# mLSTM state recurrence: one backward pass for both directions' state contributions, the forward state carried along in the output pass

## The chip, the core and the metric

The kernel runs on one core of a Trainium2 chip. The metric is the device time of one execution in microseconds, the median of several runs. One core has five engines with an instruction queue each: TensorE (PE: matrix products and transposes), VectorE (DVE), ScalarE (ACT), GpSimd (POOL) and SyncE (SP, which here issues most DMA transfers). They run side by side and wait for each other through semaphores. SBUF is the on-chip memory, PSUM the small memory into which PE writes and from which DVE and ACT can read.

## The reference, cut to what matters

Two layers of a hybrid block with three token mixers side by side: Fourier, bidirectional mLSTM, attention. 1024 latent and 256 context tokens, width 1024, all in float32. The change is in the mLSTM alone: 4 heads of dimension 96, run forward and backward over the tokens, context first in both. In layer 0 the context tokens' outputs are needed too, in layer 1 (the last) only the latents'.

```python
def mlstm_chunkwise(q, k, v, li, lf, state):
    def step(carry, inp):
        C, n, m = carry
        ...
        s = jnp.einsum("bhtd,bhsd->bhts", qb, kb) * w_intra
        num = jnp.einsum("bhts,bhsv->bhtv", s, vb) + w_inter[..., None] * jnp.einsum("bhtd,bhdv->bhtv", qb, C)
        den = s.sum(axis=-1) + w_inter * jnp.einsum("bhtd,bhd->bht", qb, n)
        h = num / jnp.maximum(jnp.abs(den), jnp.exp(-m_t))[..., None]
        ...
        C_new = decay[..., None, None] * C + jnp.einsum("bhs,bhsd,bhsv->bhdv", wk, kb, vb)
        n_new = decay[..., None] * n + jnp.einsum("bhs,bhsd->bhd", wk, kb)
        return (C_new, n_new, m_new), h
...
        fwd_c, bwd_c = mlstm_inputs(mqc, mkc, mvc, mgc, conv_qk[l], b_gates[l])
        fwd, bwd = mlstm_inputs(mq, mk, mv, mg, conv_qk[l], b_gates[l])
        hcf, st_f = mlstm_direction(fwd_c, zero, False)
        hcb, st_b = mlstm_direction(bwd_c, zero, True)
        hf, _ = mlstm_direction(fwd, st_f, False)
        hb, _ = mlstm_direction(bwd, st_b, True)
        y_m = mlstm_output(hf, hb, mo, g_mlstm[l])
```

## The kernel before

The kernel cuts the 1280 tokens into ten chunks of 128: 0 to 7 are latents, 8 and 9 context. `order[0]` is the forward order 8, 9, 0, ..., 7, and `order[1]` the backward order 9, 8, 7, ..., 0. The state of a head and direction is a 96x97 matrix: C, and n as its 97th column, since v has a column of ones. The stabilisers, weights (`wkT`) and decays (`decb`) of all chunks are worked out earlier, so that only sums and products of C are left here.

`mlstm()` is a Python generator with two passes.

The **state pass** (L825 to L853) takes 9 positions x 2 directions = 18 steps a layer. One step loads the keys of a chunk (`kc`, 96 x 4 x 128) and its values (`vc`), transposes the four heads' keys on PE (L834) into a PSUM tile, copies it with ACT into `tm` (L836), multiplies the values by the weights on POOL (L839, into a buffer with the tag `Mb`), and forms four products of 97 columns on PE (L842) in a second PSUM tile. DVE adds decay times previous state, head by head (L850, which reads the product from PSUM; the states use the tags `qw` forward and `Wb` backward), and the new state is written to DRAM (`dC`, L852). After each step the generator yields.

The **output pass** (from L875) takes a chunk at a time, 0 to 9 in layer 0 and 0 to 7 in layer 1. It loads keys, queries (`qc`), values and the output gate (`mo`), forms the scores of four heads (L885), and copies them (L887, `ssb`). Then, for each direction, it loads the masks `Mb` and `Wb` (L896), builds the weights with POOL (L897), ACT and DVE (L901, `tm`), scales the queries on POOL (L906, `qw`), loads the state before the chunk (`Cp`), and accumulates the outputs of weights and state in one PSUM tile (L912, L914). DVE divides them by the denominator: `dn` (L918 to L920) and `hd` (L922). The sum of both directions is normalised by `tail()` (L854 to L872) one chunk later: a POOL sum (L856), a small Newton iteration for the root on DVE (L175 to L187), the products L863 and L865 (`mo`), and three transposes on PE (L868).

None of this runs by itself. The generator is side work of the attention: the list `bg` at the start of the attention stage pulls it once between each of 23 pieces (keys, the first block's queries, its twelve score tiles L1005 with their maxima L1006, the row maximum L1012 and L1015, values). Then the loop over key tiles (L1140 scores, L1142 exponential, L1143 product with the values) calls `side_work()`, which pulls it at a rate set by a quota (`nm_`, the expected count of steps). Both use the PSUM tag `l`, of which there are two tiles. The order on each engine is decided when the program is built, by a list scheduler with priorities; the engines then run their queues in order.

Tags matter in what follows: a tile with a tag takes one of `bufs` buffers, and waits for the last use of the tile that had the buffer before. The state pass and the output pass share `kc`, `vc`, `tm`, `Mb`, `qw` and `Wb`, two buffers each.

Of the kernel before, what the change touches and what calls it, by code (L numbers as in the profile page):

```python
# [9 lines left out]
ALU = mybir.AluOpType  # L10
# [53 lines left out]
def build(tc, A, out, dbg=None):  # L64
    nc = tc.nc
# [40 lines left out]
    V, S, G, PE = nc.vector, nc.scalar, nc.gpsimd, nc.tensor  # L106
# [12 lines left out]
    ident = T(cst, [128, 128], tag="cst")  # L119
# [98 lines left out]
    dC = DT("dC", [2, 10, 96, 388])  # L218
# [206 lines left out]
    order = [[8, 9, 0, 1, 2, 3, 4, 5, 6, 7], [9, 8, 7, 6, 5, 4, 3, 2, 1, 0]]  # L425

    late, R1 = [], [None]
    for l in range(2):
# [286 lines left out]
        def tok(ci):  # L715
            return slice(ci * 128, (ci + 1) * 128)
# [96 lines left out]
        def mlstm(mlp_):  # L813
# [8 lines left out]

            dkh = dk.rearrange("(h d) t -> d h t", h=4)
            dqh = dq.rearrange("(h d) t -> d h t", h=4)
            prev = [None, None]  # L825
            for p in range(9):
                for d in range(2):
                    ci = order[d][p]
                    kc = T(mlp_, [96, 4, 128], tag="kc", bufs=2)
                    nc.sync.dma_start(kc, dkh[:, :, tok(ci)])  # L830
                    vc = load_v(ci)
                    ps = T(psL, [128, 512], tag="l")
                    for h in range(4):
                        PE.transpose(ps[:, h * 96:(h + 1) * 96], kc[:, h, :], ident[:96, :96])  # L834
                    kt = T(mlp_, [128, 512], tag="tm", bufs=2)
                    S.copy(kt[:, :384], ps[:, :384])  # L836
                    wcol = wkT[:, 64 * d + ci:64 * d + ci + 31:10]
                    wv = T(mlp_, [128, 4, 128], tag="Mb", bufs=2)
                    G.tensor_tensor(wv[:, :, :97], vc, wcol.unsqueeze(2).to_broadcast([128, 4, 97]), ALU.mult)  # L839
                    pc = T(psL, [128, 512], tag="l")  # L840
                    for h in range(4):
                        PE.matmul(pc[:96, h * 97:(h + 1) * 97], kt[:, h * 96:(h + 1) * 96], wv[:, h, :97], start=True, stop=True)  # L842
                    C = T(mlp_, [96, 4, 128], tag=("qw", "Wb")[d], bufs=2)
                    pv = pc[:96, :388].rearrange("p (h e) -> p h e", h=4)
                    if p == 0:
                        S.copy(C[:, :, :97], pv)
                    else:
                        for h in range(4):
                            dcol = 40 * d + 10 * h + ci
                            V.scalar_tensor_tensor(C[:, h, :97], prev[d][:, h, :97], decb[:, dcol:dcol + 1], pv[:, h], ALU.mult, ALU.add)  # L850
                    prev[d] = C
                    nc.sync.dma_start(dC[d, ci].rearrange("p (h e) -> p h e", h=4), C[:, :, :97])  # L852
                    yield  # L853
            def tail(ci, hs, mo):  # L854
                hsum = hs[0]
                G.tensor_tensor(hsum, hs[0], hs[1], ALU.add)  # L856
# [15 lines left out]
                nc.sync.dma_start(dy[256:640].rearrange("(i p) t -> p i t", p=128)[:, :, tok(ci)], ym)  # L872

            pend = None
            for ci in range(10 if ctx_all else 8):  # L875
                kc = T(mlp_, [96, 4, 128], tag="kc", bufs=2)
                nc.sync.dma_start(kc, dkh[:, :, tok(ci)])
                qc = T(mlp_, [96, 4, 128], tag="qc", bufs=2)
                nc.sync.dma_start(qc, dqh[:, :, tok(ci)])
                vc = load_v(ci)  # L880
                mo = T(mlp_, [128, 384], tag="mo", bufs=2)
                nc.sync.dma_start(mo, dv[tok(ci), 384:768])
                sp = T(psL, [128, 512], tag="l")
                for h in range(4):
                    PE.matmul(sp[:, h * 128:(h + 1) * 128], kc[:, h, :], qc[:, h, :], start=True, stop=True)  # L885
                ssb = T(mlp_, [128, 512], tag="ssb")
                S.copy(ssb, sp)  # L887
                yield
                hs = []
                for d in range(2):  # L890
                    Mb = T(mlp_, [128, 4, 128], tag="Mb", bufs=2)
                    Wb = T(mlp_, [96, 4, 128], tag="Wb", bufs=2)
                    for src, dst, np_ in ((dM, Mb, 128), (dW, Wb, 96)):
                        v_ = src[64 * d:64 * d + 40].rearrange("(h c) t -> h c t", h=4)[:, ci, :]
                        nc.sync.dma_start(dst, v_.unsqueeze(0).to_broadcast([np_, 4, 128]))
                    tm = T(mlp_, [128, 4, 128], tag="tm", bufs=2)  # L896
                    G.tensor_tensor(tm, msk[:, d].unsqueeze(1).to_broadcast([128, 4, 128]), Mb, ALU.subtract)  # L897
                    for h in range(4):
                        col = 64 * d + 10 * h + ci
                        S.activation(tm[:, h], tm[:, h], AF.Exp, bias=aT[:, col:col + 1])  # L900
                    V.tensor_tensor(tm.rearrange("p h t -> p (h t)"), tm.rearrange("p h t -> p (h t)"), ssb, ALU.mult)  # L901
                    first = ci == order[d][0]
                    if not first:
                        pi = order[d][order[d].index(ci) - 1]
                        qw = T(mlp_, [96, 4, 128], tag="qw", bufs=2)
                        G.tensor_tensor(qw, qc, Wb, ALU.mult)  # L906
                        Cp = T(mlp_, [96, 4, 97], tag="Cp", bufs=2)
                        nc.sync.dma_start(Cp, dC[d, pi].rearrange("p (h e) -> p h e", h=4))
                    po = T(psL, [128, 512], tag="l")
                    for h in range(4):  # L910
                        o = po[:, h * 97:(h + 1) * 97]
                        PE.matmul(o, tm[:, h], vc[:, h], start=True, stop=first)  # L912
                        if not first:
                            PE.matmul(o, qw[:, h], Cp[:, h], start=False, stop=True)  # L914
                    pv = po[:, :388].rearrange("p (h e) -> p h e", h=4)
                    dn = T(mlp_, [128, 4], tag="dn", bufs=2)
                    fl = flT[:, 64 * d + ci:64 * d + ci + 31:10]
                    V.scalar_tensor_tensor(dn, pv[:, :, 96], -1.0, fl, ALU.mult, ALU.max)  # L918
                    V.tensor_tensor(dn, pv[:, :, 96], dn, ALU.max)
                    V.reciprocal(dn, dn)  # L920
                    hd = T(mlp_, [128, 4, 96], tag=f"hd{d}", bufs=2)
                    V.tensor_tensor(hd, pv[:, :, 0:96], dn.unsqueeze(2).to_broadcast([128, 4, 96]), ALU.mult)  # L922
                    hs.append(hd)
                    yield
                    if d == 1 and pend is not None:
                        tail(*pend)
                        yield
                pend = (ci, hs, mo)
# [175 lines left out]
                        quota["g"] = None  # L1104
                        break

        nm_ = 18 + 4 * (10 if ctx_all else 8) - len(bg) + 1
        nf_ = (7 if ctx_all else 4) * 2 + 1
        quota = dict(m=0.0, f=0.0, g=None, rm=nm_ / (tot * RM[l]), rf=nf_ / (tot * RF))
        ending = None  # L1110
# [593 lines left out]
```

## Time and profile before

| | us |
|---|---|
| median of 3 runs | 3073.31 (3073.06 to 3073.51) |
| profiled execution, its own time | 3063.51 |
| its span, first to last instruction | 3061.7 |
| granted PE clock, mean | 0.960 |
| attention stage of layer 0: first state transposes (L834) | at 360.41 |
| first mask product of its output pass (L897) | at 424.88 |
| the same two in layer 1 | at 1966.31 and 2042.04 |
| last transposes of `tail()` in layer 1 (L868) | at 2171.3 |

The profile is of one execution. A row of a timeline gives start and length in us, engine, source line, operation, what it writes and reads, shape and count, and in brackets how long the engine had been idle ahead of it and what ended that. A table of windows gives, for each stretch, the busy time of every engine out of its length (with the number of instructions), the granted PE clock and the DMA share. `PE` is the product stream, `PEld` the loads of weights, which run beside it. A float32 product appears as two records on PE, so that `x8` is a group of four. Lines of the kernel before are L1 to L1703; the changed kernel has its own numbers, higher by up to 27 in this part.

### The profile page before, as it was taken

What the parts mean: (1) busy time and instruction counts of PE and PEld (TensorE: products, weight loads), DVE (VectorE), ACT (ScalarE), POOL (GpSimd) and SP (SyncE); (2) the same over time, 40 slices, a digit from 0 to 9 for tenths busy, and PEclk for the clock granted to TensorE, in tenths of its full rate; (3) what the DMA queues carried; (4) which work ended last, traced back from release to release, by engine and by line L of the source; (5) the groups of instructions that cost most, each with busy time, mean ns of one, the idle gap of its engine ahead of it and who ended that gap; (6) DMA issues with size and microseconds to landing.
All of it is one profiled execution on the core that took longest, in us unless ns stands there. A gap on an engine that the chain in (4) does not pass through costs nothing. (4 is left out here: it accounts for less than half of the span.)

```text
span 3061.7 us, 40347 instructions
## 1 busy us (share of the span) xinstructions
PE 2861.2 (93%) x14152; PEld 2306.0 (75%) x14152; DVE 1982.2 (65%) x3708; ACT 1176.6 (38%) x2283; POOL 1050.2 (34%) x935
## 2 busy tenths in 40 slices
PE   7998989989989999999999999899999899989996
PEld 7887866656768888788887787866657688868885
DVE  7769567632488767777777627448533854468887
ACT  3322244442343333333344533245333543434444
POOL 4212133111464444221225333224123675413334
PEclk7999998999989999999999999899999899999998
DMA  6514576223335444732121212455134343352321
GB/s 233 165 58 134 144 171 163 83 82 104 114 132 197 161 154 152 285 117 90 55 93 40 111 42 84 118 146 154 61 101 137 121 147 115 108 196 92 110 90 55
DMA packets 277871, 376.43 MB, mean 123 GB/s; under 512 B 63396, under 2 KB 154468, under 8 KB 276004
## 3 DMA queue, kind: packets, MB, share of 16 engines
q1 hardware_dynamic: 274788, 366.51, 38.1%
q0 software_dynamic: 576, 4.20, 0.4%
q10 hardware_dynamic: 2304, 3.15, 0.3%
q8 instruction: 112, 1.84, 0.2%
q14 instruction: 91, 0.75, 0.1%
HBM read 283.74 MB, written 90.02 MB: 122 GB/s over the span
## 5 line engine op out<-in xcount | busy, mean ns | idle before, releaser
L138 PE MATMUL mm<-A,wr 128*128 128x512 f32 (+1 forms) x840 | 316.5, 379 | 19.0 <-ACT rb L673 10.8
L135 PE MATMUL mm<-A 128*128 128x512 f32 (+1 forms) x654 | 251.0, 389 | 10.9 <-DVE A L148 8.5
L136 PE MATMUL mm<-A 128*128 128x512 f32 (+1 forms) x654 | 242.8, 387 | 0.3 <-DVE A L148 0.3
L134 PE MATMUL mm<-A 128*128 128x512 f32 (+1 forms) x654 | 237.6, 387 | 5.7 <-ACT A L147 4.5
L148 POOL TENSOR_TENSOR wr<-wf,wr 128x512 fp32r<-128x512 f32 x88 | 122.0, 1396 | 258.8 <-ACT wr L147 199.9
L143 PE MATMUL mm<-A,wr 128*128 128x512 f32 (+1 forms) x520 | 196.1, 378 | 4.6 <-POOL A L148 2.1
L138 PEld LDWEIGHTS mm<-A,wr 128*128 128x128 f32 x840 | 161.5, 193 | 51.5 <-ACT rb L673 12.5
L138 PE MATMUL mm<-A,c 128*128 128x512 f32 (+1 forms) x520 | 184.3, 356 | 15.4 <-ACT c L147 13.3
L144 PE MATMUL mm<-A,wr 128*128 128x512 f32 (+1 forms) x520 | 193.5, 373 | 0.0
L1143 PE MATMUL v<-PT,Vt 128*97 128x512 f32 (+1 forms) x336 | 176.7, 610 | 12.5 <-ACT PT L1142 12.5
L143 PE MATMUL mm<-A,c 128*128 128x512 f32 (+1 forms) x520 | 184.9, 356 | 3.1 <-DVE A L148 2.3
L144 PE MATMUL mm<-A,c 128*128 128x512 f32 (+1 forms) x520 | 183.9, 354 | 0.8 <-DVE c L148 0.8
L235 DVE SCALAR_TENSOR_TENSOR junk<-wf,t 128x512 bf16<-128x512 f32 x192 | 131.3, 684 | 74.0 <-DMA wf<-in_w_mt 70.6
L1140 PE MATMUL s<-Q,KT 97*128 97x512 f32 (+1 forms) x336 | 174.0, 606 | 0.4 <-ACT Q L1016 0.4
L147 ACT ACTIVATE A<-wr 128x512 fp32r<-128x512 f32 x188 | 114.2, 625 | 147.7 <-PE mm L135 59.2
L147 ACT ACTIVATE A<-A 128x512 fp32r<-128x512 f32 x174 | 106.9, 625 | 158.3 <-PE mm L135 85.1
L1142 ACT ACTIVATE PT<-s 128x512 f32<-128x512 f32 (+1 forms) x168 | 97.9, 584 | 153.7 <-PE s L1140 153.3
L148 DVE TENSOR_TENSOR A<-wr,A 128x512 fp32r<-128x512 f32 x146 | 128.3, 891 | 42.8 <-ACT A L147 27.7
L135 PEld LDWEIGHTS mm<-A 128*128 128x128 f32 x654 | 123.4, 189 | 39.5 <-DVE A L148 11.9
L134 PEld LDWEIGHTS mm<-A 128*128 128x128 f32 x654 | 122.7, 188 | 31.1 <-ACT A L147 7.0
L136 PEld LDWEIGHTS mm<-A 128*128 128x128 f32 x654 | 123.5, 189 | 24.8 <-DVE A L148 0.7
L138 PE MATMUL mm<-wr,A 128*128 128x256 f32 x464 | 134.0, 289 | 6.6 <-ACT rb L673 4.7
(481 smaller groups left out, 8016.8 us busy)
## 6 DMA issues: line engine op xcount, KB each, us to landing
wf<-in_w_mt SPq DMA_DIRECT2D x96, 256.0 KB
x<-in_w_up SPq DMA_DIRECT2D x40, 512.0 KB
r<-in_w_up SPq DMA_DIRECT2D x38, 512.0 KB
wr<-in_w_dn SPq DMA_DIRECT2D x36, 512.0 KB
gt<-in_w_mt SPq DMA_DIRECT2D x64, 256.0 KB
da<-wf SPq DMA_DIRECT2D x64, 256.0 KB
da<-p SPq DMA_DIRECT2D x64, 256.0 KB
wf<-in_w_in SPq DMA_DIRECT2D x56, 256.0 KB
```

The source lines that it names most:

```text
L134: PE.matmul(ps, lh, rh, start=first, stop=False, skip_group_check=True)
L135: PE.matmul(ps, lh, rl, start=False, stop=False, skip_group_check=True)
L136: PE.matmul(ps, ll, rh, start=False, stop=last, skip_group_check=True)
L138: PE.matmul(ps, lh, rh, start=first, stop=False)
L143: PE.matmul(ps, lh, rl, start=False, stop=False)
L144: PE.matmul(ps, ll, rh, start=False, stop=last)
L147: (hi or S).activation(dst[0], src, AF.Copy) if (hi is None or hi is S) else hi.tensor_copy(dst[0], src)
L148: (lo or G).tensor_tensor(dst[1], src, f32(dst[0]), ALU.subtract)
L235: V.scalar_tensor_tensor(junk, f, 1.0, cb[w], ALU.mult, ALU.mult, accum_out=(ga, modT[l])[kh][:, w, j:j + 1])
L1140: PE.matmul(ps[:, :nq], K[:, tok(kt)], Q[:, :nq], start=True, stop=True)
L1142: S.activation(PT[:, :nq], ps[:, :nq], AF.Exp, scale=scale)
L1143: PE.matmul(po[:97, :nq], Vt[kt // 2][:, kt % 2, h % 2], PT[:, :nq], start=i == 0, stop=i == len(kts) - 1)
```

## The change

The state pass now takes the ten chunks once, in backward order. For each it makes one load of keys and values, one set of transposes, two POOL products (one for each direction, side by side in a tile with its own tag, `wv`), and four PE products of 194 columns in two PSUM tiles. The forward half of each product, not yet summed, is copied by ACT (`fw`, tag `Cp`, now four buffers) and written to `dC[0, ci]`. The backward half is summed with the decayed state as before (L853, tag `Cf`) and written to `dC[1, ci]`. It yields twice a chunk.

The forward state is summed up in the output pass by `forward()`: it loads the chunk's contribution from `dC[0, ci]` and adds decay times the state so far with four DVE instructions (L869), whose tensors all lie in SBUF. It is called behind the products of direction 0. So that the state is at hand, the output pass of layer 0 now runs in the order 8, 9, 0, ..., 7; in layer 1, which has no outputs for 8 and 9, `forward()` runs for these two ahead of the loop.

Per layer there are 10 state steps in place of 18: 40 transposes in place of 72, 40 products of 194 columns in place of 72 of 97, 10 loads of kc and vc each in place of 18, 20 POOL products in place of 18, 32 DVE instructions that read PSUM in place of 64, 32 new ones that read SBUF alone, and 20 ACT copies of forward halves that are new.

```diff
-            prev = [None, None]
-            for p in range(9):
+            prev = None
+            for ci in order[1]:
+                kc = T(mlp_, [96, 4, 128], tag="kc", bufs=2)
+                nc.sync.dma_start(kc, dkh[:, :, tok(ci)])
+                vc = load_v(ci)
...
+                wv = T(mlp_, [128, 4, 2, 97], tag="wv", bufs=2)
                 for d in range(2):
...
                     wcol = wkT[:, 64 * d + ci:64 * d + ci + 31:10]
-                    wv = T(mlp_, [128, 4, 128], tag="Mb", bufs=2)
-                    G.tensor_tensor(wv[:, :, :97], vc, wcol.unsqueeze(2).to_broadcast([128, 4, 97]), ALU.mult)
+                    G.tensor_tensor(wv[:, :, d], vc, wcol.unsqueeze(2).to_broadcast([128, 4, 97]), ALU.mult)
+                yield
+                fw = T(mlp_, [96, 4, 97], tag="Cp", bufs=4)
+                C = T(mlp_, [96, 4, 97], tag="Cf", bufs=2)
+                for hp in range(2):
                     pc = T(psL, [128, 512], tag="l")
-                    for h in range(4):
-                        PE.matmul(pc[:96, h * 97:(h + 1) * 97], kt[:, h * 96:(h + 1) * 96], wv[:, h, :97], start=True, stop=True)
-                    C = T(mlp_, [96, 4, 128], tag=("qw", "Wb")[d], bufs=2)
...
+                    pv = pc[:96, :388].rearrange("p (h d e) -> p h d e", h=2, d=2)
+                    for h in range(2 * hp, 2 * hp + 2):
+                        PE.matmul(pc[:96, 194 * (h % 2):194 * (h % 2) + 194], kt[:, h * 96:(h + 1) * 96], wv[:, h].rearrange("p d e -> p (d e)"), start=True, stop=True)
+                    S.copy(fw[:, 2 * hp:2 * hp + 2], pv[:, :, 0])
+                    if prev is None:
+                        S.copy(C[:, 2 * hp:2 * hp + 2], pv[:, :, 1])
+                    elif ci:
+                        for h in range(2 * hp, 2 * hp + 2):
+                            dcol = 40 + 10 * h + ci
+                            V.scalar_tensor_tensor(C[:, h], prev[:, h], decb[:, dcol:dcol + 1], pv[:, h % 2, 1], ALU.mult, ALU.add)
+                if ci != 7:
+                    nc.sync.dma_start(dC[0, ci].rearrange("p (h e) -> p h e", h=4), fw)
+                if ci:
+                    nc.sync.dma_start(dC[1, ci].rearrange("p (h e) -> p h e", h=4), C)
+                prev = C
+                yield
+
+            def forward(ci, C):
+                lc = T(mlp_, [96, 4, 97], tag="Cp", bufs=4)
+                nc.sync.dma_start(lc, dC[0, ci].rearrange("p (h e) -> p h e", h=4))
+                if C is None:
+                    return lc
+                n_ = T(mlp_, [96, 4, 97], tag="Cf", bufs=2)
+                for h in range(4):
+                    dcol = 10 * h + ci
+                    V.scalar_tensor_tensor(n_[:, h], C[:, h], decb[:, dcol:dcol + 1], lc[:, h], ALU.mult, ALU.add)
+                return n_
...
-            for ci in range(10 if ctx_all else 8):
+            Cf = None
+            if not ctx_all:
+                for ci in order[0][:2]:
+                    Cf = forward(ci, Cf)
+            for ci in order[0] if ctx_all else order[0][2:]:
...
-                        Cp = T(mlp_, [96, 4, 97], tag="Cp", bufs=2)
-                        nc.sync.dma_start(Cp, dC[d, pi].rearrange("p (h e) -> p h e", h=4))
+                        if d:
+                            Cp = T(mlp_, [96, 4, 97], tag="Cp", bufs=4)
+                            nc.sync.dma_start(Cp, dC[d, pi].rearrange("p (h e) -> p h e", h=4))
+                        else:
+                            Cp = Cf
...
+                    if d == 0 and ci != 7:
+                        Cf = forward(ci, Cf)
...
-        nm_ = 18 + 4 * (10 if ctx_all else 8) - len(bg) + 1
+        nm_ = 20 + 4 * (10 if ctx_all else 8) - len(bg) + 1
```

Three places show how the queues move. The first is PE's queue at the start of the attention stage of layer 0: `l_...` are PSUM tiles of the mLSTM, `m_...` those of attention, and a row is an instruction, or a run of them, in the order of its queue (the score tiles L1005 are left out). Before:

```order
L834 MATMUL l_3497<-cst_60,kc_3492 128x96 x4
...
L842 MATMUL l_3506<-Mb_3504,tm_3502 96x97
L834 MATMUL l_3548<-cst_60,kc_3543 128x96 x4
L842 MATMUL l_3506<-Mb_3504,tm_3502 96x97 x3
...
L842 MATMUL l_3557<-Mb_3555,tm_3553 96x97 x4
L834 MATMUL l_3576<-cst_60,kc_3571 128x96 x4
...
L842 MATMUL l_3585<-Mb_3583,tm_3581 96x97
L834 MATMUL l_3607<-cst_60,kc_3602 128x96 x4
L842 MATMUL l_3585<-Mb_3583,tm_3581 96x97 x3
L842 MATMUL l_3616<-Mb_3614,tm_3612 96x97 x4
L834 MATMUL l_3638<-cst_60,kc_3633 128x96 x4
L1015 MATMUL m_4037<-cst_60,m_746_4035 1x128
```

After (L832 is the transpose, L846 the product, L1032 the score tile, L1042 the row maximum's transpose):

```order
L832 MATMUL l_3497<-cst_60,kc_3492 128x96 x4
L1032 MATMUL m_3645<-x_588_3481,Qr_3615 128x512
...
L1032 MATMUL m_3830<-x_588_3481,Qr_3615 128x512
L846 MATMUL l_3538<-wv_3504,tm_3502 96x194 x2
L846 MATMUL l_3543<-wv_3504,tm_3502 96x194 x2
L1032 MATMUL m_3848<-x_588_3481,Qr_3615 128x256
L832 MATMUL l_3561<-cst_60,kc_3556 128x96 x4
L1042 MATMUL m_3869<-cst_60,m_701_3867 1x128
```

Ahead of the row maximum stood four groups of products and five of transposes; now there are one chunk's products and two groups of transposes, and eleven of the twelve score tiles stand ahead of the products.

The second is SP's queue at the same place, with the loads of keys (`kc`), values (`vc`) and the output pass's masks (`Mb`, `Wb`). Before:

```order
L830 DMA kc_3492<-dk_80 96x4x128
L830 DMA kc_3543<-dk_80 96x4x128
...
L820 DMA vc_3545<-dv_81 128x4x96
L830 DMA kc_3571<-dk_80 96x4x128
L820 DMA vc_3494<-dv_81 128x4x96
```

After:

```order
L917 DMA Mb_3941<-dM_89 128x4x128
L917 DMA Mb_3973<-dM_89 128x4x128
L917 DMA Wb_3942<-dW_90 96x4x128
L828 DMA kc_3492<-dk_80 96x4x128
L828 DMA kc_3556<-dk_80 96x4x128
L901 DMA qc_3919<-dq_79 96x4x128
L917 DMA Wb_3974<-dW_90 96x4x128
L820 DMA vc_3558<-dv_81 128x4x96
L820 DMA vc_3494<-dv_81 128x4x96
```

The first masks of the output pass are now loaded ahead of the first keys.

The third is DVE's queue in one chunk of the output pass of layer 0. `dn` is the denominator and `hd` the output of one direction, `y` the Newton iterate, `mo` the product of the chunk before, and `mx` the maxima of attention. Before:

```order
L918 SCALAR_TENSOR_TENSOR dn_4697<-l_4688,flT_1253 128x4
L185 TENSOR_TENSOR rs_t_4797<-y_962_4793 128x4
L919 TENSOR_TENSOR dn_4697<-l_4688,dn_4697 128x4
L186 TENSOR_TENSOR rs_t_4797<-rs_t_4797,rs_h_4794 128x4
L920 RECIPROCAL dn_4697<-dn_4697 128x4
L187 SCALAR_TENSOR_TENSOR y_962_4793<-rs_t_4797,y_962_4793 128x4
L922 TENSOR_TENSOR hd_936_4701<-l_4688,dn_4697 128x384
```

After:

```order
L945 SCALAR_TENSOR_TENSOR dn_4604<-l_4588,flT_1253 128x4
L869 SCALAR_TENSOR_TENSOR Cf_4755<-Cf_4599,decb_1254,Cp_4753 96x97 x4
L1033 TENSOR_REDUCE mx_5048<-m_5049 128x1
L883 SCALAR_TENSOR_TENSOR mo_4367<-mo_4367,hd_862_4424 128x384
L946 TENSOR_TENSOR dn_4604<-l_4588,dn_4604 128x4
L945 SCALAR_TENSOR_TENSOR dn_4646<-l_4637,flT_1253 128x4
...
L947 RECIPROCAL dn_4604<-dn_4604 128x4
...
L949 TENSOR_TENSOR hd_912_4608<-l_4588,dn_4604 128x384
```

The four instructions of the forward state stand between the first and the second instruction of the denominator of direction 0, ahead of the product `mo` of the chunk before.

More of the change, by code (lines that the diff above doesn't have):

```diff
@@ L824, in mlstm @@
             dqh = dq.rearrange("(h d) t -> d h t", h=4)
-            prev = [None, None]
-            for p in range(9):
-                for d in range(2):
[L828 to L832, printed above, removed]
-                    for h in range(4):
-                        PE.transpose(ps[:, h * 96:(h + 1) * 96], kc[:, h, :], ident[:96, :96])
-                    kt = T(mlp_, [128, 512], tag="tm", bufs=2)
-                    S.copy(kt[:, :384], ps[:, :384])
-                    wcol = wkT[:, 64 * d + ci:64 * d + ci + 31:10]
-                    wv = T(mlp_, [128, 4, 128], tag="Mb", bufs=2)
-                    G.tensor_tensor(wv[:, :, :97], vc, wcol.unsqueeze(2).to_broadcast([128, 4, 97]), ALU.mult)
-                    pc = T(psL, [128, 512], tag="l")
-                    for h in range(4):
-                        PE.matmul(pc[:96, h * 97:(h + 1) * 97], kt[:, h * 96:(h + 1) * 96], wv[:, h, :97], start=True, stop=True)
-                    C = T(mlp_, [96, 4, 128], tag=("qw", "Wb")[d], bufs=2)
[L844 to L853, printed above, removed]
@@ new lines, in mlstm @@
+            prev = None
[3 more added lines that the diff above has]
+                vc = load_v(ci)
+                ps = T(psL, [128, 512], tag="l")
+                for h in range(4):
+                    PE.transpose(ps[:, h * 96:(h + 1) * 96], kc[:, h, :], ident[:96, :96])
+                kt = T(mlp_, [128, 512], tag="tm", bufs=2)
+                S.copy(kt[:, :384], ps[:, :384])
+                wv = T(mlp_, [128, 4, 2, 97], tag="wv", bufs=2)
+                for d in range(2):
+                    wcol = wkT[:, 64 * d + ci:64 * d + ci + 31:10]
+                    G.tensor_tensor(wv[:, :, d], vc, wcol.unsqueeze(2).to_broadcast([128, 4, 97]), ALU.mult)
[3 more added lines that the diff above has]
+                for hp in range(2):
+                    pc = T(psL, [128, 512], tag="l")
+                    pv = pc[:96, :388].rearrange("p (h d e) -> p h d e", h=2, d=2)
[14 more added lines that the diff above has]
+                yield
@@ new lines, in forward @@
+            def forward(ci, C):
[4 more added lines that the diff above has]
+                n_ = T(mlp_, [96, 4, 97], tag="Cf", bufs=2)
+                for h in range(4):
+                    dcol = 10 * h + ci
+                    V.scalar_tensor_tensor(n_[:, h], C[:, h], decb[:, dcol:dcol + 1], lc[:, h], ALU.mult, ALU.add)
+                return n_
```

## The prediction

> **What bounds the kernel now.** I read the page's busy times first, then the busy time by stage in the stretches where the diff's lines run.
>
> ```profile
> PE 2861.2 (93%) x14152; PEld 2306.0 (75%) x14152; DVE 1982.2 (65%) x3708; ACT 1176.6 (38%) x2283; POOL 1050.2 (34%) x935
> ...
> core 0: us, PE busy (x) PEld busy (x) DVE busy (x) ACT busy (x) POOL busy (x), PEclk, DMA share, GB/s
> ...
> 390.00:420.00 30.00, 30.00 (x187) 21.19 (x185) 18.21 (x58) 12.26 (x24) 8.63 (x18) 1.00 0.76 172
> ...
> 480.00:510.00 30.00, 26.32 (x138) 17.96 (x137) 24.29 (x68) 13.96 (x36) 12.22 (x13) 0.94 0.56 157
> ...
> 2080.00:2110.00 30.00, 28.14 (x134) 18.03 (x133) 28.55 (x68) 13.96 (x36) 12.57 (x12) 0.94 0.63 159
> ```
>
> PE is the bound overall, and wholly so in 390–420, where the state pass runs beside attention: there a PE microsecond saved is one gained. In the output pass (480–510, 2080–2110) PE has holes (26.32 and 28.14 of 30), while DVE is at 24 to 28.5. The change takes work from the first kind of stretch and puts some into the second. Nothing outside the attention stages changes.
>
> **PE work of the state pass.** The PE timeline inside the full stretch (start, length, engine, line):
>
> ```profile
> 393.22 0.84 PE L842 MATMUL l<-Mb,tm 128*96 128x97 f32 x8
> 393.90 0.50 PE L834 MATMUL l<-cst,kc 96*128 96x96 f32 x4
> 394.23 1.02 PE L1143 MATMUL v<-PT,Vt 128*97 128x512 f32 x2
> 395.09 1.02 PE L1140 MATMUL s<-Q,KT 97*128 97x512 f32 x2
> ```
>
> From start to start a step's four products (eight records) take 0.68 us, its transposes 0.33 us, a pair of 512-column records 0.86 us (0.84 ns a column). A layer has 18 such steps: 18 x 1.01 = 18.2 us. Afterwards it has 10, with the same transposes and eight records of 194 columns. No row shows that width. By columns alone they take 8 x 194 x 0.84 ns = 1.30 us; by twice the present record 1.36 us; I take 1.33. So 10 x 1.66 = 16.6 us, 1.6 less a layer: **-3.2 us** for both (-2.6 to -3.8).
>
> **The start of the stage.** PE and DVE at the start of layer 0 and layer 1:
>
> ```profile
> 360.41 0.52 PE L834 MATMUL l<-cst,kc 96*128 96x96 f32 x4 [1.51 <-DMA kc<-dk]
> 364.02 1.86 PE L1005 MATMUL m<-x,Qr 96*128 96x512 f32 x4 [3.09 <-ACT Qr L996]
> 366.80 0.64 PE L842 MATMUL l<-Mb,tm 128*96 128x97 f32 x2 [0.91 <-POOL Mb L839]
> ...
> 375.66 0.27 PE L1015 MATMUL m<-cst,m 128*1 128x128 f32 x1
> ...
> 364.85 2.21 DVE L1006 TENSOR_REDUCE mx<-m 128x1 f32<-128x512 f32 x4 [1.59 <-PE m L1005]
> ...
> 1975.44 1.29 DVE L1006 TENSOR_REDUCE mx<-m 128x1 f32<-128x512 f32 x2 [1.59 <-PE m L1005]
> 1976.76 1.46 DVE L751 TENSOR_TENSOR fd<-up 128x256 f32<-128x256 f32 x2
> ...
> 1978.48 1.06 DVE L751 TENSOR_TENSOR fd<-um 128x256 f32<-128x256 f32 x2
> ...
> 1980.99 0.98 DVE L850 SCALAR_TENSOR_TENSOR qw<-qw,decb,l 96x97 f32<-96x97 f32 x4
> ...
> 1990.39 0.16 DVE L1012 TENSOR_REDUCE m<-mx 128x4 f32<-128x12 f32 x1
> ...
> 365.90 1.63 POOL L839 TENSOR_TENSOR Mb<-vc,wkT 128x388 f32<-128x388 f32 x2 [3.73 <-DMA mo<-dv]
> ...
> 357.12 0.97 SPq L830 DMA_DIRECT2D kc<-dk  x2
> ```
>
> The first attention block needs twelve score tiles (L1005) and their maxima (L1006, 2.21/4 = 0.55 us each) before the row maximum (L1015). In layer 0, four groups of products and five of transposes stand among them on PE, and L842 and L1005 wait for each other's buffers and for POOL. In the new order eleven score tiles run through first. Twelve reduces from 364.85 end near 371.5: L1015 comes 4.2 us sooner. By then before had done 4 x 0.68 + 5 x 0.33 = 4.4 us of state work and had 13.8 left; the changed kernel has done 1.33 + 2 x 0.33 = 2.0 and has 14.6 left. Net -4.2 + 0.8 = -3.4, of which -1.6 is counted above: -1.8.
>
> In layer 1, four groups like the one at 1980.99 delay the reduces. Without them the reduces, with four L751 (1.46 + 1.06 = 2.5 us), end near 1975.44 + 6.6 + 2.5 = 1984.6, 5.8 before L1012. But three product pairs now stand on PE ahead of the row maximum, each needing two POOL products (L839, 1.63/2 = 0.82 us each) in time. I count half of the 5.8, -2.9, of which -1.6 is counted already: -1.3 (the state work left then is about equal: before has 12 x 0.68 + 11 x 0.33 = 11.8, the changed kernel 7 x 1.66 = 11.6).
>
> Against this, SP now issues two Mb loads and a Wb load ahead of the first kc, and one more Wb ahead of vc. At about half a microsecond each (0.97/2) that is 1.5 to 2 us. kc may come that late without harm, since PE waits until 364.02 for Qr anyway; the vc load's product is first needed late. If this cover failed it would cost up to 2 us a layer. I take **-3 us** for both layers, between -6 and +4.
>
> **From the state pass to the output pass.** The Mb and Wb buffers are shared with the state pass, so the first mask loads wait until it lets them go:
>
> ```profile
> 424.88 1.28 POOL L897 TENSOR_TENSOR tm<-msk,Mb 128x512 f32<-128x512 f32 x1 [8.10 <-DMA Mb<-dM]
> ...
> 429.56 0.74 PE L912 MATMUL l<-vc,tm 128*128 128x97 f32 x2 [2.22 <-DVE tm L901]
> ...
> 437.39 0.46 PE L914 MATMUL l<-Cp,qw 96*128 96x97 f32 x2 [0.89 <-POOL qw L906]
> ...
> 2051.47 0.74 PE L914 MATMUL l<-Cp,qw 96*128 96x97 f32 x2 [3.31 <-POOL qw L906]
> ```
>
> With tiles of their own (wv, Cf) for the state pass, these loads go out at the start of the stage, tens of microseconds early. The waits are 2.22 + 0.89 + 3.31 = 6.4 us. What would be late next is the chain POOL mask, ACT exp, DVE product itself, so not all goes: **-5 us** (-6.4 to 0).
>
> **The forward state in the output pass.** DVE's 32 state instructions per layer that now stand there (L869) read two SBUF tensors; those removed (L850) read PSUM. POOL is busy there 12.22 of 30 us, 0.41. What that does to DVE (statistics of two lines in ns; then DVE, POOL and PE around one chunk):
>
> ```profile
> L850 DVE SCALAR_TENSOR_TENSOR qw<-qw,decb,l x64: 302/306/315, 374.2 to 2040.0; 96x97 f32<-96x97 f32 x64
> ...
> L865 DVE SCALAR_TENSOR_TENSOR mo<-mo,hd x18: 545/558/2744, 457.2 to 2168.5; 128x384 f32<-128x384 f32 x18
> ...
> 489.59 0.16 DVE L187 SCALAR_TENSOR_TENSOR y<-rs_t,y 128x4 f32<-128x4 f32 x1
> 489.95 0.16 DVE L918 SCALAR_TENSOR_TENSOR dn<-l,flT 128x4 f32<-128x4 f32 x1 [0.20 <-PE l L914]
> ...
> 491.09 2.43 DVE L186 TENSOR_TENSOR rs_t<-rs_t,rs_h 128x4 f32<-128x4 f32 x1
> ...
> 493.55 1.26 DVE L187 SCALAR_TENSOR_TENSOR y<-rs_t,y 128x4 f32<-128x4 f32 x1
> ...
> 489.77 1.27 POOL L897 TENSOR_TENSOR tm<-msk,Mb 128x512 f32<-128x512 f32 x1 [5.31 <-PE l L912]
> ...
> 496.48 0.52 PE L868 MATMUL l<-cst,mo 128*128 128x128 f32 x3 [1.44 <-DVE dn L919]
> ...
> 498.78 1.92 PE L1143 MATMUL v<-PT,Vt 128*97 128x512 f32 x2
> ```
>
> The same L187 takes 0.16 us alone and 1.26 us beside a POOL product; L186 takes 2.43 across two of them. L865, both inputs in SBUF, goes up to 2744 ns; L850, with one in PSUM, never leaves 302 to 315. So the four L869 of a chunk cost about 1.0 us free (the L850 group of four took 0.98) and 4 x 1.27 = 5.1 us if each waits out a POOL instruction. With POOL busy 0.41 of the time, one such wait at that chance gives 1.0 + 0.41 x 1.27 = 1.5; I take that.
>
> The DVE order shows twelve groups of L869 (six a layer, the rest clear of it) between a chunk's first dn and its hd, with the tail's mo product (now L883) behind. What PE feels is at the tail's transposes, by the line's waits:
>
> ```profile
> L868 PE MATMUL l<-cst,mo x54: 270/272/447, 457.8 to 2171.3; 128*128 128x128 f32 x54
> its engine sat idle before it (us, times) until:
>   DVE m L1012: 4.8, 1
>   DVE dn L919: 3.5, 2
>   DVE dn L918: 1.6, 2
>   DVE mo L865: 0.3, 1
> ```
>
> In 6 of 18 chunks PE already waits there for DVE; in those, whatever is put ahead adds in full, elsewhere the queued attention matmuls (0.86 us a pair) hide it. So 12 x 6/18 = 4 groups x 1.5 = 6 us. After such a wait an L1143 pair took 1.92 us where 1.02 is usual; two more of these make 2 us. **+8 us**; the ends are 0 (all hidden) and 4 x 5.1 + 2 = 22.
>
> The Trainium skill, "SBUF — State Buffer", section "🔬 SBUF: two separate sides", says that a DVE operation with two SBUF inputs and a GpSimd operation that reads SBUF exclude each other for a whole instruction, the first to start holding the ports. The rows agree (0.16 against 1.26), and by that rule alone a group could cost the 5.1; without it, 1.0.
>
> **Costed at nothing.** The fw copies (L847 on) go to ACT, busy 12 to 14 of 30, beside attention matmuls; if the two PSUM buffers of the state pass came free late, each of ten chunks could lose some tenths, inside the range. The forward loads come from dC parts written long before. SP issues 31 fewer transfers.
>
> **Sum.** -3.2 - 3 - 5 + 8 = -3.2 on the profiled 3063.51 us. The median 3073.31 lies 9.8 above that run; the same offset gives **3070.1 us**, 0.1% faster, which no measurement of this kernel tells from no change (that takes about 0.2%, 6.1 us).
>
> **Rivals.**
> - *The forward step is hidden.* For it: the L1143 and L1140 pairs between the products and the tail, and twelve of eighteen chunks with no wait at L868. Against: DVE at 28.55 of 30 in 2080–2110. Then -3.2 - 3 - 6.4 = -12.6: 3060.7. Chance 0.22.
> - *The lock decides.* L869 is ready with the first dn, just when POOL starts its run of mask and qw products (the run from 489.77, the first dn at 489.95); each of the four waits out one. From about 3 us per group on the gain is used up (4 x 3 + 2 = 14 against 11.2). At 5.1: 22 - 11.2 = +10.8, 3084. Here DVE becomes the bound of the output pass. The skill's rule above would give this. Chance 0.20.
> - *The early loads do harm.* Mb and Wb ahead of kc and vc delay the start by 2 us a layer, and the transition's waits only change their cause: -3.2 + 4 + 0 + 8 = +8.8, 3082. For it: the 1.51 us wait on kc. Against: the 3.09 us wait on Qr behind it. Chance 0.08.
> - *Only PE's work counts:* the order of the rest is as good as before, -3.2, the same 3070. It lies within the forecast.
>
> **How the numbers follow.** The forecast has 0.50, with its own range 3062 to 3078. About 0.10 of it lies below 3067.2 and none above 3079.4. Faster: 0.22 + 0.10 = 0.32. Slower: 0.20 + 0.07 = 0.27. Same: 0.41. The range reaches from just below the first rival to the second: 3059 to 3085.
>
> **What would show it.** Right: state products of about 0.16 us a record, L1042 (the row maximum) 3 to 4 us sooner after the stage's first transposes, no waits over 1 us on the first mask and qw products, and L869 groups between 1 and 2 us with longer waits at L886 to L888 (the tail's transposes). Wrong: L869 at 0.3 us everywhere and no new PE waits (first rival); L869 above 0.7 us on average (second); later wv products at the start (third).

## The result and the profile after

| | before | after |
|---|---|---|
| median of 7 runs each, us | 3070.66 (3067.28 to 3073.51) | 3088.45 (3080.50 to 3101.34) |
| ratio, 95% interval | | 1.0061 (1.0042 to 1.0079) |
| profiled execution, own time / span, us | 3063.51 / 3061.7 | 3083.63 / 3081.9 |
| granted PE clock, mean | 0.960 | 0.957 |

The change makes the kernel 0.61% slower, some 19 us, where -3 us was forecast. 0.001 of ratio is 3.1 us in all that follows.

The profile after, part by part in the prediction's order. First the page's head of the changed kernel:

```profile
span 3081.9 us, 39846 instructions
## 1 busy us (share of the span) xinstructions
PE 2869.7 (93%) x13960; PEld 2305.5 (75%) x13960; DVE 1998.1 (65%) x3708; ACT 1179.7 (38%) x2307; POOL 1047.7 (34%) x923
```

PE has 192 records fewer and is busy 8.5 us longer. The mean granted clock is 0.957 where it was 0.960, which on 2861 us is about 9 us, so the clock alone can account for it.

The PE timeline of the changed kernel in the state pass (columns as in the prediction):

```profile
409.09 1.48 PE L846 MATMUL l<-wv,tm 128*96 128x194 f32 x8
410.41 1.02 PE L1170 MATMUL v<-PT,Vt 128*97 128x512 f32 x2
411.27 1.02 PE L1167 MATMUL s<-Q,KT 97*128 97x512 f32 x2
```

A chunk's products take 1.32 us from start to start (410.41 - 409.09); 1.33 was the estimate. Where the granted clock was 0.50, as in the next view at 374.78, they take 2.4 to 2.7.

The start of layer 0's stage in the changed kernel, PE and then SP's queue:

```profile
366.67 0.87 PE L832 MATMUL l<-cst,kc 96*128 96x96 f32 x4 [6.71 <-DMA kc<-dk]
368.62 5.42 PE L1032 MATMUL m<-x,Qr 96*128 96x512 f32 x11 [1.08 <-ACT Qr L1023]
374.78 2.90 PE L846 MATMUL l<-wv,tm 128*96 128x194 f32 x8 [0.74 <-POOL vc L819]
...
378.62 0.37 PE L1042 MATMUL m<-cst,m 128*1 128x128 f32 x1
...
358.20 0.95 SPq L917 DMA_DIRECT2D Mb<-dM  x2
359.20 0.50 SPq L917 DMA_DIRECT2D Wb<-dW  x1
359.74 1.00 SPq L828 DMA_DIRECT2D kc<-dk  x2
```

The order is as foreseen: the row maximum comes 11.95 us after the first transposes (15.25 before). But these transposes wait 6.71 us for the first keys, where it was 1.51. The issue of the masks holds up that of kc by only 1.45 us (0.95 + 0.50). The larger part comes behind it: from the issue of kc to the transposes it is 6.93 us (359.74 to 366.67), where it was 3.29 (357.12 to 360.41). Counted from the end of the PE work before the wait, the row maximum comes 18.66 us later, for 16.76 before.

The waits of PE in the first attention stage (waited for, total us, times, longest):

```profile
PE l L832 <- DMA kc<-dk: 6.7, 1, 6.7
PE l L886 <- DVE dn L945: 5.0, 2, 2.6
PE m L1032 <- ACT Qr L1023: 4.8, 2, 3.7
PE l L886 <- DVE mo L883: 4.3, 2, 3.4
...
PE m L1042 <- DVE m L1039: 2.7, 1, 2.7
PE m L1032 <- DVE mx L1033: 2.6, 3, 1.6
PE l L886 <- DVE dn L946: 1.0, 1, 1.0
PE l L937 <- DVE tm L923: 0.9, 1, 0.9
```

The mask waits of the transition are nearly gone (L937 0.9). New are the waits for DVE at the score tiles (L1032) and row maxima (L1042) of attention: 5.3 us, where there were none. Those at the tail's transposes (L886) add up to 10.3 for 9.0 before. In layer 1 the first kind is 7.4 us (2.8 before) and the second 5.4 (1.2). All of PE's waits for DVE at these lines come to 28.5 us in both layers, for 13.0 before.

The forward sums in the changed kernel: the line's lengths in ns (least, median, greatest) and what DVE stood idle for ahead of it (us, times), then DVE, POOL and PE around one chunk of layer 0:

```profile
L869 DVE SCALAR_TENSOR_TENSOR Cf<-Cf,decb,Cp x56: 301/308/2629, 443.6 to 2159.4; 96x97 f32<-96x97 f32 x56
...
  DMA Cp<-dC: 6.7, 3
...
497.17 0.16 DVE L945 SCALAR_TENSOR_TENSOR dn<-l,flT 128x4 f32<-128x4 f32 x1
497.25 5.11 DVE L869 SCALAR_TENSOR_TENSOR Cf<-Cf,decb,Cp 96x97 f32<-96x97 f32 x4
502.28 0.68 DVE L1033 TENSOR_REDUCE mx<-m 128x1 f32<-128x512 f32 x1
502.88 0.54 DVE L883 SCALAR_TENSOR_TENSOR mo<-mo,hd 128x384 f32<-128x384 f32 x1
503.35 0.15 DVE L946 TENSOR_TENSOR dn<-l,dn 128x4 f32<-128x4 f32 x1
...
496.88 1.38 POOL L919 TENSOR_TENSOR tm<-msk,Mb 128x512 f32<-128x512 f32 x1 [7.02 <-PE l L937]
498.23 1.29 POOL L928 TENSOR_TENSOR qw<-qc,Wb 96x512 f32<-96x512 f32 x1
499.48 1.26 POOL L919 TENSOR_TENSOR tm<-msk,Mb 128x512 f32<-128x512 f32 x1
...
500.75 1.26 POOL L928 TENSOR_TENSOR qw<-qc,Wb 96x512 f32<-96x512 f32 x1
...
503.01 0.49 PE L1032 MATMUL m<-x,Qr 96*128 96x512 f32 x1 [1.63 <-DVE mx L1033]
...
506.19 1.64 PE L1170 MATMUL v<-PT,Vt 128*97 128x512 f32 x2
507.62 1.92 PE L1167 MATMUL s<-Q,KT 97*128 97x512 f32 x2
```

This is the mechanism of the loss. Four sums that take 0.31 us each alone occupy DVE for 5.11 us (1.14, 2.56, 1.33 and 0.30), until POOL's run of four products ends at 502.01. A maximum of attention stands behind them, PE runs dry for want of its tile, and the matmuls that follow run at half speed (1.92 for the usual 1.02). Over both layers the 64 instructions take 48.2 us, added up from the trace, 0.75 each where 0.31 is free; 23 of them, in 13 of the 16 groups, take over 0.4 us. For three groups DVE also stood idle until the loaded contribution was there, 6.7 us in all.

### The profile page after: what moved, and what is told of

Its sections match the earlier page's. It is cut to its first block, busy times and chain, and to the rows that moved or that the text cites. A ratio compares the mean times of both kernels' runs of the same rounds, so it can differ in the third digit from the quotient of the medians.

```text
span 3081.9 us, 39846 instructions
## 1 busy us (share of the span) xinstructions
PE 2869.7 (93%) x13960; PEld 2305.5 (75%) x13960; DVE 1998.1 (65%) x3708; ACT 1179.7 (38%) x2307; POOL 1047.7 (34%) x923
## 4 chain that ended last, share of the span: by engine, by line
PE 55%; DVE 20%; DMA 10%; issue 7%; POOL 3%; ACT 3%; SPq 1%; DVEq 0%; POOLq 0%; ACTq 0%
PE mm L138 8%; PE mm L144 6%; PE mm L143 6%; PE s L1167 4%; PE mm L135 4%; PE v L1170 4%; PE mm L136 4%; PE mm L134 3%; DMA wf<-in_w_mt 3%; DVE junk L235 3%; DVE A L148 2%; DVE ac L677 2%; PE mm L140 2%; PE mm L141 2%; PE mm L1495 2%
## 5 line engine op out<-in xcount | busy, mean ns | idle before, releaser
L138 PE MATMUL mm<-A,wr 128*128 128x512 f32 (+1 forms) x840 | 316.2, 379 | 18.7 <-ACT rb L673 10.4
L1170 PE MATMUL v<-PT,Vt 128*97 128x512 f32 (+1 forms) x336 | 176.8, 611 | 13.6 <-ACT PT L1169 13.5
L1033 DVE TENSOR_REDUCE mx<-m 128x1 f32<-128x512 f32 (+1 forms) x200 | 107.8, 586 | 68.0 <-PE m L1032 67.9
```

The lines of the kernel that those rows point to most:

```text
L138: PE.matmul(ps, lh, rh, start=first, stop=False)
L1033: V.tensor_reduce(Pr[h, qb][:, qs, i:i + 1], ps[:, :n], AX.X, ALU.max)
L1170: PE.matmul(po[:97, :nq], Vt[kt // 2][:, kt % 2, h % 2], PT[:, :nq], start=i == 0, stop=i == len(kts) - 1)
```

## The experiments

Three theories stood at the start. **A**, the sums wait for POOL's instructions ("the lock" from here on, as in the prediction's rival) and hold up what is behind them on DVE. **B**, the early mask loads delay the stage's first keys and values. And as rival to A, the mere place of the sums in DVE's queue, or their latency. Ratios are to the kernel before on the same chip, from 6 to 12 runs each.

### No forward sums

```diff
-                n_ = T(mlp_, [96, 4, 97], tag="Cf", bufs=2)
-                for h in range(4):
-                    dcol = 10 * h + ci
-                    V.scalar_tensor_tensor(n_[:, h], C[:, h], ...)
-                return n_
+                return lc
```

> The changed kernel with the forward sums (L869) left out: the state contribution of one chunk is used as the state, so the outputs are not the reference's; loads, products and order stay. Theory A (forward sums in front of dn and mo on DVE, stretched by POOL's port use, hold up the tail's transposes): 9 to 13 us off the changed kernel's time, ratio to before about 1.002 to 1.003. Theory B (the early Mb and Wb loads delay kc and vc at the stage's start): ratio stays at 1.005 to 1.006.

0.9952 (0.9937 to 0.9968). The forward sums cost 1.0061 - 0.9952 = 0.011, some 33 us, and without them the rest of the change gains 15 us. As theory A has it, but some three times the 9 to 13 us that it expected.

### The same sums, read from PSUM

```diff
-V.scalar_tensor_tensor(n_[:, h], C[:, h], decb[...], lc[:, h], ...)
+V.scalar_tensor_tensor(n_[:, h], C[:, h], decb[...], lc[:, h] if src is None else src[:, h], ...)
...
-Cf = forward(ci, Cf)
+Cf = forward(ci, Cf, po[:96, :388].rearrange("p (h e) -> p h e", h=4))
```

> The changed kernel with the forward sums reading the product's PSUM tile (po) in place of the loaded contribution in SBUF inside the output loop, so the outputs are not the reference's; the number of DVE instructions and their place stay. Theory A with the lock as the cause: L869 falls from a mean of 0.75 us to 0.31 and the time with it, ratio 1.002 to 1.004, close to the run without sums. If only the place in DVE's queue counts and not the lock: ratio 1.005 to 1.006. Theory B: 1.005 to 1.006.

`po` is the tile of the chunk's outputs, so the states are wrong and only the time is of use. 0.9940 (0.9922 to 0.9958), the same as without sums, and below the 1.002 to 1.004 that theory A expected. The line's lengths in this run, then one group and the POOL products beside it:

```profile
L869 DVE SCALAR_TENSOR_TENSOR Cf<-Cf,decb,l x56: 299/305/315, 465.3 to 2141.2; 96x97 f32<-96x97 f32 x56
...
508.49 0.99 DVE L869 SCALAR_TENSOR_TENSOR Cf<-Cf,decb,l 96x97 f32<-96x97 f32 x4 [0.16 <-PE l L939]
509.40 0.15 DVE L945 SCALAR_TENSOR_TENSOR dn<-l,flT 128x4 f32<-128x4 f32 x1
...
508.31 1.27 POOL L919 TENSOR_TENSOR tm<-msk,Mb 128x512 f32<-128x512 f32 x1 [9.59 <-PE l L937]
509.54 1.27 POOL L928 TENSOR_TENSOR qw<-qc,Wb 96x512 f32<-96x512 f32 x1
```

As many DVE instructions, called at the same place in the program, with one operand in PSUM, cost nothing that can be measured. Added up from the trace, POOL was busy during 18.4 of their 19.6 us, and none was stretched; so it is the second SBUF operand that makes them wait for POOL. PE's waits for DVE at L886, L1032 and L1042 fall from 28.5 us to 13.5. Two more things differ in this run. On DVE the sums now stand just ahead of the chunk's first dn, no longer just behind it; as they delay the same denominators, their mere place does not explain the loss. And the sums in the loop no longer wait for a load. The 6.7 us that DVE stood idle for that in the changed kernel can't explain much of it, since PE has no wait over 0.3 us close behind (430 to 450 and 2070 to 2082); but the runs don't price it by itself.

This pair also shows how the cost splits. The two attention stages (from the first state transposes to the last L1170) by windows, with the changed kernel first and the run with PSUM operands second:

```profile
366.67:760.12 393.45, 355.74 (x1583) 235.03 (x1583) 211.02 (x529) 158.02 (x373) 100.10 (x109) 0.93 0.39 107
1983.56:2307.10 323.54, 303.43 (x1322) 196.13 (x1323) 185.67 (x447) 135.57 (x303) 86.75 (x94) 0.94 0.40 112
```

```profile
368.13:735.31 367.18, 341.31 (x1583) 225.69 (x1583) 198.21 (x529) 157.82 (x373) 100.31 (x109) 0.96 0.41 115
1967.15:2271.96 304.81, 291.16 (x1322) 188.86 (x1323) 175.20 (x445) 136.44 (x303) 86.40 (x94) 0.97 0.42 118
```

The stages are 26.3 and 18.7 us longer in the changed kernel. PE has the same records in both, but is busy 14.4 and 12.3 us longer at a clock of 0.93 and 0.94 instead of 0.96 and 0.97; only 11.8 and 6.5 us are idle time. So 26.7 of the 45.0 us, more than half, is PE working at a lower clock, and not PE waiting. (These are single executions; the runs give 0.012, 37 us.)

### Masks loaded after the state pass again

```diff
-wv = T(mlp_, [128, 4, 2, 97], tag="wv", bufs=2)
+wv = T(mlp_, [128, 4, 2, 97], tag="Mb", bufs=2)
...
-C = T(mlp_, [96, 4, 97], tag="Cf", bufs=2)
+C = T(mlp_, [96, 4, 128], tag="Wb", bufs=2)[:, :, :97]
...
-Mb = T(mlp_, [128, 4, 128], tag="Mb", bufs=2)
+Mb = T(mlp_, [128, 776], tag="Mb", bufs=2)[:, :512].rearrange("p (h t) -> p h t", h=4)
```

> The changed kernel with wv in the Mb buffers and the backward state in the Wb buffers, so that the masks load only after the state pass, as before the change. Theory B: the kc wait at the start falls from 6.7 and 4.3 us to under 2, the stage starts about 5 us (layer 0) and 2 us (layer 1) sooner; the transition's waits (6.4 us before) come back for about 5 us: ratio 1.004 to 1.006. Theory A: no change at the start that matters, the transition's waits come back: 1.007 to 1.008.

1.0048 (1.0032 to 1.0064), not told apart from the change itself. That is what theory B expected (1.004 to 1.006), and below what theory A alone did (1.007 to 1.008). PE's wait at the first transposes fell from 6.7 and 4.3 us to 1.5 and 0.2; that the transition lost about as much was not measured by itself.

### Early mask loads in the kernel before

```diff
-wv = T(mlp_, [128, 4, 128], tag="Mb", bufs=2)
+wv = T(mlp_, [128, 4, 97], tag="wv", bufs=2)
...
-C = T(mlp_, [96, 4, 128], tag=("qw", "Wb")[d], bufs=2)
+C = T(mlp_, [96, 4, 97], tag=("Ca", "Cb")[d], bufs=2)
```

> The kernel before with buffers of their own for wv and the states (tags wv, Ca, Cb), so that only the early mask loads come in. Theory B: the wait for the first kc grows from 1.5 us to 5 or 6 and the start loses 4 to 5 us a layer, the transition gains 5: ratio 1.000 to 1.002. Theory A: the start hides it, ratio 0.998 to 0.999.

0.9996 (0.9983 to 1.0010): no change. The time alone doesn't choose between theory B (1.000 to 1.002) and theory A (0.998 to 0.999); PE's waits up to the transition of each layer do:

```profile
PE l L834 <- DMA kc<-dk: 6.9, 1, 6.9
...
PE l L834 <- DMA kc<-dk: 6.4, 1, 6.4
```

The wait for the first kc rises to 6.9 and 6.4 us (1.5 and 1.7 before), while the transition's mask waits (6.4 us) go. Behind the first transposes the two stages are 5.0 and 5.7 us shorter than before (377.43 for 382.42 and 315.85 for 321.59), which makes up for it. Early loads alone are a loss at one end and a gain behind it.

### First masks gated behind two chunks

The masks should load early, but not ahead of the first keys. Only the first two chunks' `wv` and `C` take the mask buffers:

```diff
-wv = T(mlp_, [128, 4, 2, 97], tag="wv", bufs=2)
+wv = T(mlp_, [128, 4, 2, 97], tag="Mb" if ci in order[1][:2] else "wv", bufs=2)
...
-C = T(mlp_, [96, 4, 97], tag="Cf", bufs=2)
+C = T(mlp_, [96, 4, 128], tag="Wb", bufs=2)[:, :, :97] if ci in order[1][:2] else T(mlp_, [96, 4, 97], tag="Cf", bufs=2)
...
-Mb = T(mlp_, [128, 4, 128], tag="Mb", bufs=2)
+Mb = T(mlp_, [128, 776], tag="Mb", bufs=2)[:, :512].rearrange("p (h t) -> p h t", h=4)
```

> The changed kernel with only that gating of the first mask loads; the forward sums stay on DVE from SBUF. Lock theory: still slower than before, 1.003 to 1.006. If the early loads were the main cause: 1.000 or below.

1.0024 (1.0010 to 1.0038). 0.0037, some 11 us, better than the change, and still slower than before. That is just below the lock theory's 1.003 to 1.006, and above the 1.000 expected if the early loads were the main cause. PE at the start of layer 0's stage in this run:

```profile
361.85 0.52 PE L832 MATMUL l<-cst,kc 96*128 96x96 f32 x4 [1.31 <-DMA kc<-dk]
365.55 2.46 PE L1032 MATMUL m<-x,Qr 96*128 96x512 f32 x6 [3.18 <-ACT Qr L1023]
```

The keys are there again after 1.31 us.

### The sum on ACT and POOL, without and with the gate

```diff
-                    V.scalar_tensor_tensor(n_[:, h], C[:, h], ...)
+                    S.activation(n_[:, h], C[:, h], AF.Copy, scale=decb[:96, dcol:dcol + 1])
+                G.tensor_tensor(n_, n_, lc, ALU.add)
```

> The changed kernel with the forward sum off DVE: ACT scales the state by the decay (four copies), one POOL addition of 96x388 adds the contribution. Lock theory: the sums no longer stand in DVE's queue and the time falls to that of the run without sums plus what the POOL addition (about 1 us, between the mask products of direction 0 and 1) costs: ratio 0.995 to 1.000. If the forward sum's latency itself, on whatever engine, were the cause: 1.004 or more.

> As fwd_ap, with the first two chunks' wv and backward state in the Mb and Wb buffers, so that the first mask loads can't start ahead of the first keys and values, but come well before the output pass. If the early loads cost the start what the waits for kc show (6.7 and 4.3 us, under 2 before): 0.002 below fwd_ap, 0.993 to 0.998. If the delay is hidden behind Qr and the maxima: the same as fwd_ap.

1.0046 (1.0027 to 1.0065) without the gate and 0.9989 (0.9975 to 1.0004) with it. The first misses what the lock theory expected (0.995 to 1.000) and lies where the rival put it: the addition now stands in POOL's queue among the mask products, on which the next weights depend. Which part of the loss is that queue wasn't separated. The second, too, lies just above what it expected (0.993 to 0.998), but the gate is worth more than the 0.002 forecast: 0.0057 here.

### Idle sums in the kernel before

```diff
+                    if d == 0 and not first:
+                        n_ = T(mlp_, [96, 4, 97], tag="Cf", bufs=2)
+                        for h in range(4):
+                            dcol = 10 * h + ci
+                            V.scalar_tensor_tensor(n_[:, h], Cp[:, h], decb[:, dcol:dcol + 1], Cp[:, h], ALU.mult, ALU.add)
```

> The kernel before with four idle DVE instructions of the forward sum's form (two SBUF inputs, results used by nothing) behind direction 0's products in each chunk that has a state: 16 groups, and nothing else changed. Lock theory: they alone cost what the forward sums cost, 1.006 to 1.012, with lengths up to 2.5 us each. If the loss comes from the forward state's dependence or the new chunk order: under 1.003.

1.0079 (1.0057 to 1.0102). There are 17 groups, not 16. Nothing uses their results and no order of chunks changes; the kernel before becomes 24 us slower by them alone. Their lengths, and what DVE stood idle for ahead of them:

```profile
L919 DVE SCALAR_TENSOR_TENSOR Cf<-Cp,decb x68: 298/308/1681, 388.8 to 2186.7; 96x97 f32<-96x97 f32 x68
...
  DMA Cp<-dC: 9.8, 5
```

Both the dependence and the new chunk order are thereby ruled out as needed for a loss. But these 24 us are not the lock's alone. Only 12 of the 68 are stretched, and together they take 32.5 us, some 11.5 more than free; DVE stood idle 9.8 us ahead of five groups until Cp was loaded, and the sums can hold the two Cp buffers longer. How the loss divides among these was not separated.

### All forward sums ahead of the output pass

On the gated kernel; states written back to `dC` and loaded as before the change:

```diff
-            if not ctx_all:
-                for ci in order[0][:2]:
-                    Cf = forward(ci, Cf)
+            for i, ci in enumerate(order[0][:9]):
+                Cf = forward(ci, Cf)
+                if i:
+                    nc.sync.dma_start(dC[0, ci].rearrange("p (h e) -> p h e", h=4), Cf)
...
-                    if d == 0 and ci != 7:
-                        Cf = forward(ci, Cf)
```

> The gated kernel with the forward sums of all chunks done in a row between the state pass and the output pass (same DVE instructions, both inputs in SBUF), each state written back to dC and loaded as Cp, as before the change. Lock theory: there POOL has little to do, so L869 stays near 0.31 us and no dn waits behind it; the merged state pass and the gating keep their gain: ratio 0.990 to 0.996. If the SBUF form alone costs, wherever it stands: 1.002, as the gated kernel.

(With them the program yields three times more a layer, and `nm_` grows by 3.) 1.0012 (0.9996 to 1.0027): the lock goes, the gain doesn't come. The lock theory expected 0.990 to 0.996, and by its time alone the run fits the other expectation, a cost of the SBUF form wherever it stands (1.002). The sums and one of PE's waits in layer 0's transition:

```profile
L869 DVE SCALAR_TENSOR_TENSOR Cf<-Cf,decb,Cp x56: 305/309/318, 430.0 to 2067.3; 96x97 f32<-96x97 f32 x56
...
444.74 0.74 PE L939 MATMUL l<-Cp,qw 96*128 96x97 f32 x2 [2.22 <-DMA Cp<-dC]
```

L869 is down to 0.31 us as expected, with POOL busy during 1.2 of their 20.4 us, so the form alone doesn't stretch the sums. But the states now go out to DRAM and come back in the middle of the transition, and PE waits 2.22 us for one of them, with slow matmuls behind. How much of the missing gain this is was not measured by itself.

### The contribution brought to PSUM by ACT

On the gated kernel; the sums stay on DVE in the output loop:

```diff
+                pl = T(psL, [128, 512], tag="l")[:96, :388].rearrange("p (h e) -> p h e", h=4)
+                S.copy(pl, lc)
...
-                    V.scalar_tensor_tensor(n_[:, h], C[:, h], decb[...], lc[:, h], ALU.mult, ALU.add)
+                    V.scalar_tensor_tensor(n_[:, h], C[:, h], decb[...], pl[:, h], ALU.mult, ALU.add)
```

> The gated kernel with the contribution copied by ACT into a PSUM tile of the tag l, from which DVE takes it in the same place of the output loop: the right sum without a lock. Lock theory: L869 at 0.31 us, 10 us or more gained on the gated kernel; the third tenant of the two l tiles costs some of it: ratio 0.993 to 1.000. If the two l tiles decide: 1.002 or more.

> As gated_actps, with the forward sum called behind direction 1's output instead of direction 0's products, so that it doesn't take the l tile that direction 1 needs. Lock theory: no worse than gated_actps, 0.992 to 0.999. If the l tiles don't matter: the same as gated_actps.

> As gated_actps without the gating of the mask loads: the changed kernel, but for the contribution coming to DVE through PSUM. If the gating is worth what it was with the lock (gated against the changed kernel: 0.0037; gated_ap against fwd_ap: 0.0057): 0.997 to 1.000. If it is worth nothing once the lock is gone (the run with sums from po reached 0.994 without it): 0.993 to 0.996.

The gated kernel with it: **0.9941** (0.9926 to 0.9956), 18 us faster than before, 0.0083 (some 25 us) faster than the gated kernel and 0.012 faster than the change. Called behind direction 1 instead: 0.9952 (0.9935 to 0.9969), not told apart. Without the gate: 0.9999 (0.9984 to 1.0015), so the gate is worth 0.0058 here too; that it would be worth nothing without the lock has fallen. The lengths in the best run:

```profile
L871 DVE SCALAR_TENSOR_TENSOR Cf<-Cf,decb,l x56: 302/305/314, 456.0 to 2136.1; 96x97 f32<-96x97 f32 x56
```

One more ACT copy and one more PSUM tile a chunk cost far less than the lock. This pair alone doesn't show that the operand made the gain, though: in the best run the scheduler put the sums mostly ahead of the Newton steps, where POOL was busy during only 1.3 of their 19.6 us. Called behind direction 1 they stood beside POOL during 12.3 of 19.4 us, were no longer than 0.32 us either, and the time was about the same. And the ungated run lies 0.006 above the run that read `po`, which needs neither copy nor tile nor the load; so these have a price, which wasn't taken apart.

## Why the prediction was wrong, point by point

- **PE work of the state pass, -3.2: right in its unit price.** 1.32 us a chunk's products for 1.33, at full clock; three of the 20 groups, at the starts, took 2.4 to 2.7 us at a granted clock of 0.50.
- **Start of the stage, -3: wrong in sign in layer 0, too large in layer 1.** From the first transposes to the row maximum the path became shorter about as worked out (by 3.3 us in layer 0). But counted from the end of the PE work before, the row maximum came 1.9 us later in layer 0 (18.66 for 16.76) and 0.95 sooner in layer 1 (25.01 for 25.96), where 4.2 and 2.9 sooner were forecast. The step that failed is the price of the early loads, "1.5 to 2 us", hidden behind Qr. It counted SP's issue time alone. The masks' 704 KB (two of 256 KB, one of 192 KB) were also under way ahead of kc, and the wait for kc grew by 6.71 - 1.51 = 5.2 us in layer 0 and from 1.67 to 4.34 in layer 1. The cover was there, but small: the wait for Qr fell from 3.09 to 1.08 us. The gate shows the worth of putting this right: 0.0037 to 0.0058, 11 to 18 us in three pairs of kernels.
- **Transition, -5: right in sign, and too small.** The waits went from 6.4 to 0.9 us. The early loads alone, in the kernel before, lost 5.4 and 4.7 us at the two starts by their kc waits and came out even. Behind the first transposes 5.0 and 5.7 us came back; 2.0 of that in layer 0 is the smaller wait for Qr, so how much is the transition's stays open. The sum counted the waits alone; the matmuls behind the stall in layer 1 ran slowly as well (an L912 pair 0.63 us at 2052.00, where 0.39 is usual).
- **Forward sums, +8 with an upper end of 22: right mechanism, wrong size, and it decided the result.** This is the step that failed most: they cost 33 to 37 us. Three factors of the term were off. First, a group was priced at 1.5 us, by POOL's average share of 0.41; it took 48.2/16 = 3.0, and 13 of the 16 groups were stretched. The wait isn't met by chance: the dn that the sums follow and the run of four POOL products start behind the same chunk's products, within 0.3 us of each other (497.17 and 496.88 above). The rival called this by name and had 0.20. Second, only L868's waits were counted, 4 groups of 12; the sums also stood ahead of attention's maxima, and PE waited at L1032 and L1042. Third, the clock: 2 us were set aside, and it was more than half of the cost (26.7 of 45.0 us in the profiled pair).
- **Costed at nothing: the forward loads.** They were taken to be early, and for three groups they were not: DVE stood idle 6.7 us for them. No run prices this by itself.
- **The rival "the lock decides"** had the mechanism, and put the total at +10.8 with 5.1 us a group, for +19 measured. At the 3.0 us that a group took its own sum gives +2.8, so it was too small for the same reasons: four groups counted, and 2 us for the clock. "The early loads do harm" was true as well, with 0.08. Both were priced as exclusive cases, while they came together, with a larger gain of the rest in between (0.9952 without the sums).

## What to carry to other kernels

A DVE instruction is not priced by its length alone: where its operands lie and what POOL is doing when it is released decide (0.75 us on average for 0.31), and an average share of POOL's time misleads when both start behind the same event. One operand in PSUM made the same instruction free of it. Giving a load a buffer of its own also lets it overtake: what it gets ahead of is the price, and a tag shared with just the first tiles can hold it back to the right moment.

## What the runs showed of the hardware that was not expected

In the prediction's own rows a slow pair stood behind a wait of 1.44 us. The runs show how much such pairs can add up to (26.7 us), and how little waiting comes before one. The windows of the changed kernel behind the group of 5.11 us (length, then PE's busy time, and the clock ahead of the DMA share):

```profile
502.00:506.00 4.00, 1.99 (x6) 0.94 (x7) 4.00 (x14) 0.54 (x2) 0.01 (x1) 1.00 0.60 136
506.00:510.00 4.00, 4.00 (x10) 1.98 (x10) 2.56 (x6) 1.31 (x4) 0.99 (x1) 0.57 0.95 248
```

No single wait there is longer than 1.63 us, yet after a stretch in which PE was half idle the next 4 us are granted 0.57 of the clock. The Trainium skill, "TensorE: Matmul & The Clock Gate", section "🔬 Part 1: The HAM clock gate (the "warmup" mystery)", has the slow state come after an idle window of about 3.4 us. Here it came behind a stretch that was only half idle; how much idle time it takes was not measured.
